# Three pairs of chunks block by block at a sub-layer's end, and the last output columns on other engines

## The chip, the cores and the metric

The kernel runs on one core of a Trainium2 chip. The metric is the time of one execution in device microseconds, the median of three runs. TensorE (PE in the profile, with PEld for its weight loads) multiplies matrices, VectorE (DVE), ScalarE (ACT) and GpSimd (POOL) work on the results, and SyncE (SP) issues the DMAs.

## The reference

A decoder trunk of two layers for 256 tokens of width 1024, in fp32. Each layer has an attention sub-layer (three head groups side by side) and an MLP sub-layer, and each sub-layer ends with a layer norm whose output the next sub-layer reads after a scale and a shift:

```
for l in range(DEPTH):                                   # DEPTH = 2
    mod = silu(c) @ ada_w[l] + ada_b[l]
    sh_a, sc_a, g_a, sh_m, sc_m, g_m = split(mod, 6)
    h = x * (1 + sc_a) + sh_a
    mixed = attention_groups(h @ w_in[l])                # A, B, C; width 1024
    x = layer_norm(DN_ALPHA * x + (1 + g_a) * (mixed @ w_out[l]), ln_g[l, 0], ln_b[l, 0])
    h = x * (1 + sc_m) + sh_m
    f = square(relu(h @ mlp_w1[l])) @ mlp_w2[l]          # 1024 -> 4096 -> 1024
    x = layer_norm(DN_ALPHA * x + (1 + g_m) * f, ln_g[l, 1], ln_b[l, 1])
return x
```

## The kernel before, in words

The 256 tokens are two blocks of 128 (`b` = 0, 1), the 1024 columns two halves of 512 (`h` = 0, 1). Every fp32 weight tile comes by a 1 MB DMA into one of four buffers (`raw`, issued in order by SP) and is split into a high part `whi` (ScalarE, L179) and a low part `wlo` (VectorE, or GpSimd where told, L180). A product is three matmuls: high by high, high by low, low by high. In the output projection these are `wo` (L1051 to L1053), in the MLP's second product `m2` (L1116 to L1118), each 128x512 into one of four accumulators. The split parts of a pair of chunks take four of the ten buffers `w` (128x1024 each); other pools are `u2` (eleven buffers of 128x512), `mx` (four, which also hold the MLP's activations), `P` (four) and `qk` (three).

A sub-layer ends in `transition`. The last two pairs of chunks are not done for both blocks in turn: block 0 gets its products half by half, then block 1 gets its own. While PE does block 1's, the other engines take block 0 through the norm. VectorE does `half(h)`: multiply (L405), add the residual (L409), statistics (L412); then mean and variance (L416 to L419), GpSimd's power (L420), the scaled row `P` (VectorE L427 for columns 0 to 511, ScalarE L425 and L426 for the rest), eight transposes on PE (`turn`, L454, tile `tp`), the modulation (VectorE L463, ScalarE L461), the high part of the new input `hT` (ScalarE L466) and its low part (VectorE L470). PE's next work after block 1's products is `v_tile` (L385, `mmv`), the first products of the next sub-layer for block 0, and it needs `hT`. Block 1's norm then runs beside these. Between the steps stand splits of weights for the next sub-layer: `pool_split` gives a `wlo` to GpSimd.

PE's order is made by the scheduler; the order on VectorE, ScalarE and GpSimd inside `transition` is the order of the code. This happens three times: at the end of layer 0's attention, of layer 0's MLP and of layer 1's attention. The end of layer 1's MLP is `last_norm`: block 0's last multiply and add run on GpSimd (`on_pool`, L539, 640 and then 384 columns), block 1's on VectorE (L563 and L566, two halves of 512), and SP stores the output (L535).

In the MLP the groups g = 0 to 15 of 256 inner columns follow one another: `m1(g+2)` makes activations ahead, `m2` uses those of g, and `filler` puts in steps of the next modulation vector (`gemv`: VectorE L234 on 1 MB of weights each).

Of the kernel before, what the change touches and what calls it, by code (L numbers as in the profile page):

```python
# [28 lines left out]
EARLY = 3  # L29
FO = (1, 3)  # L30
ORDER = ('kv0..21s4.3sa5.s.Acb.6.B7C..Ee', '.ts..q0412...ss3s.kva5cb.67AB.E..Ce')
GV = ('v', None, 'v', 'v', 'v')
# [88 lines left out]
def trunk_kernel(ctx: ExitStack, tc: tile.TileContext, a):  # L121
# [48 lines left out]

    SPARE = dict(P=4, qk=3, mx=4)

    def parts(t, n, eng=None, tag="w"):

        if tag == "w":
            hi, lo = (spl.tile([128, 1024], F32R, name=k, tag="w")[:, :n] for k in ("whi", "wlo"))
        else:
            hi, lo = (att.tile([128, 1024], F32R, name=k, tag=tag, bufs=SPARE[tag])[:, :n] for k in ("whi", "wlo"))
        nc.scalar.activation(hi, t, AF.Copy)  # L179
        (eng or nc.vector).tensor_tensor(lo, t, hi.bitcast(F32), op=OP.subtract)  # L180
        return hi, lo

    def split(t, rows, n):

        out = []
        for piece in pieces(t, rows, n, out):
            piece()
        return out

    def pieces(t, rows, n, out, step=None):  # L190
# [282 lines left out]
    def transition(products, accs, G, lnb, rnd, weights, spare, work):  # L473

        N = [Norm(b, accs[b], G, lnb) for b in range(2)]
        H = [MakeH(b, N[b], ROUND[rnd]) for b in range(2)]
# [52 lines left out]
    def last_norm(products, accs, G, lnb):  # L529

        N = [Norm(b, accs[b], G, lnb) for b in range(2)]
        E = mybir.EngineType

        def store(n, c0, c1):
            nc.sync.dma_start(a["out"][0, n.b * 128:(n.b + 1) * 128, c0:c1], x[:, n.b, c0:c1])  # L535

        def on_pool(n, c0, c1):
            for i, op in enumerate((OP.mult, OP.add)):
                nc.gpsimd.tensor_tensor(x[:, n.b, c0:c1], (n.r[:, c0:c1], x[:, n.b, c0:c1])[i], lnb[:, i, c0:c1], op=op)  # L539
            store(n, c0, c1)  # L540

        with tc.manual_schedule(engines={E.DVE, E.Pool}):
            n = N[0]
            for h in range(2):
                products(0, (h,))
# [7 lines left out]
            n = N[1]  # L553
            for h in range(2):
                products(1, (h,))
                n.half(h)
            n.stats()
            on_pool(N[0], 640, D)
            cuts = ((0, 512), (512, D))
            for c0, c1 in cuts:  # L560
                s = slice(c0, c1)
                o = n.halves[c0 // 512]
                nc.vector.scalar_tensor_tensor(o, o, n.mv[:, 0:1], lnb[:, 0, s], op0=OP.subtract, op1=OP.mult)  # L563
            for c0, c1 in cuts:
                s = slice(c0, c1)
                nc.vector.scalar_tensor_tensor(x[:, 1, s], n.halves[c0 // 512], n.ve[:, 1:2], lnb[:, 1, s],  # L566
                                               op0=OP.mult, op1=OP.add)
                store(n, c0, c1)

# [353 lines left out]
    for l in range(DEPTH):  # L923
# [119 lines left out]

        def wo(b, c2, hs):
            for k, h in ((k, h) for k in range(2) for h in hs):
                c = 2 * c2 + k
                hi, lo = WO[c]
                mh, ml = MX[c2][:, 0, k, b * 128:(b + 1) * 128], MX[c2][:, 1, k, b * 128:(b + 1) * 128]
                s = slice(h * 512, h * 512 + 512)
                o = accs[b][h]  # L1050
                nc.tensor.matmul(o, mh, hi[:, s], start=c == 0, stop=False)  # L1051
                nc.tensor.matmul(o, mh, lo[:, s], start=False, stop=False)  # L1052
                nc.tensor.matmul(o, ml, hi[:, s], start=False, stop=c == 7)  # L1053
# [51 lines left out]
        def load_w2(g):  # L1105
            W2[g] = split(rawload(a["mlp_w2"][l, g]), 2, 1024)

        def m2(g, b, hs):
            f = FT[g]
            t = slice(b * 128, (b + 1) * 128)  # L1110
            for i, h in ((i, h) for i in range(2) for h in hs):
                o = accs[b][h]
                s = slice(h * 512, h * 512 + 512)
                hi, lo = W2[g][i]
                first, lastk = g == 0 and i == 0, g == NG - 1 and i == 1
                nc.tensor.matmul(o, f[:, 0, i, t], hi[:, s], start=first, stop=False)  # L1116
                nc.tensor.matmul(o, f[:, 0, i, t], lo[:, s], start=False, stop=False)  # L1117
                nc.tensor.matmul(o, f[:, 1, i, t], hi[:, s], start=False, stop=lastk)  # L1118

        before = [p for g in range(EARLY) for p in w1_steps(g)]  # L1120
        end = transition(lambda b, h: [wo(b, c2, h) for c2 in (2, 3)], accs, ROUND[l, 3], lnb, (l, 2), before, SPARES[0],
                         [lambda b, g=g: m1_rows(g, b) for g in range(EARLY)])
# [4 lines left out]
        accs = [[ps.tile([128, 512], F32, name="m2", tag=t) for _ in range(2)] for t in ("acc", "sc")]  # L1127
        for g in range(NG - 2):
            with tc.issue_after(end[0]), tc.issue_after(end[1]):
                if EARLY <= g + 2 < NG:  # L1130
                    m1(g + 2)
                load_w2(g)
            for b in range(2):
                m2(g, b, (0, 1))
# [7 lines left out]
        tail = lambda b, h, m2=m2: [m2(g, b, h) for g in (NG - 2, NG - 1)]  # L1142
        if l < DEPTH - 1:
# [73 lines left out]
```

## Time and profile before

| | |
|---|---|
| median of 3 runs | 706.01 us (705.96 to 706.22) |
| the profiled execution | 706.43 us, of which its span 704.7 us |
| PE busy | 674.1 us, 96% of the span |
| VectorE, ScalarE, GpSimd busy | 492.3, 402.6, 39.1 us |
| mean granted TensorE clock | 0.991 of full speed |

The profile shows one execution. Busy times of PE overlap a little, since matmuls are pipelined: a 128x512 matmul is shown with 0.39 us, and one follows another after less.

### The profile page before, as it was taken

How to read it: one execution, taken by the hardware profiler on the slowest of the kernel's cores; microseconds unless marked ns; L12 is line 12 of the kernel's file. 1: busy time of each engine (PE TensorE's matmuls, PEld its weight loads, DVE VectorE, ACT ScalarE, POOL GpSimd, SP SyncE). 2: the span in 40 equal slices, each digit the busy share in tenths (PEclk: the TensorE clock that was granted, in tenths of full speed). 3: DMA queues.
4: the chain of work that ended last, by engine and by line, in shares of the span. 5: the costliest groups of instructions: out<-in, count | busy, mean ns of one | idle time of the engine just before them, and what ended most of it. 6: DMA issues, size and time to landing. Idle time of an engine off the chain costs nothing.

```text
span 704.7 us, 11146 instructions
## 1 busy us (share of the span) xinstructions
PE 674.1 (96%) x4284; PEld 550.9 (78%) x4284; DVE 492.3 (70%) x947; ACT 402.6 (57%) x781; POOL 39.1 (6%) x39
## 2 busy tenths in 40 slices
PE   5998899999999999999998999999999999999994
PEld 4898658458788888888878977867788888888883
DVE  3455965657799879798977976657779855555556
ACT  2345473785665546656555447598474655656550
POOL 0000000000400000000013020000220000000003
PEclk9999999999999999999999999999999999999998
DMA  9998686568459989798873757710538955555501
GB/s 337 350 353 312 224 319 231 169 236 312 162 183 363 346 309 344 283 344 327 326 262 120 282 226 274 272 39 23 183 117 294 373 214 195 212 183 180 180 0 60
DMA packets 29553, 167.68 MB, mean 238 GB/s; under 512 B 3199, under 2 KB 6683, under 8 KB 11964
## 3 DMA queue, kind: packets, MB, share of 16 engines
q1 hardware_dynamic: 29436, 166.94, 65.0%
q8 instruction: 34, 0.56, 0.3%
q14 instruction: 19, 0.16, 0.1%
q0 software_dynamic: 64, 0.02, 0.0%
HBM read 165.87 MB, written 1.08 MB: 237 GB/s over the span
## 4 chain that ended last, share of the span: by engine, by line
PE 89%; DVE 4%; ACT 3%; issue 1%; POOL 1%; DMA 1%; SPq 0%; POOLq 0%; DVEq 0%
PE mm L368 14%; PE m L1116 8%; PE m L1117 8%; PE m L1118 8%; PE mmv L385 7%; PE mm L369 7%; PE s L680 3%; PE tp L648 3%; PE gv L168 3%; PE mm L355 2%; PE mm L357 2%; PE mm L356 2%; PE wo L1051 2%; PE wo L1053 2%; PE acc L696 2%; PE wo L1052 2%
## 5 line engine op out<-in xcount | busy, mean ns | idle before, releaser
L180 DVE TENSOR_TENSOR wlo<-raw,whi 128x1024 fp32r<-128x1024 f32 (+2 forms) x166 | 196.8, 1203 | 56.5 <-ACT whi L179 54.9
L179 ACT ACTIVATE whi<-raw 128x1024 fp32r<-128x1024 f32 (+2 forms) x175 | 179.2, 1041 | 56.8 <-PE wo L1052 17.2
L368 PE MATMUL mm<-hT,whi 128*128 128x512 f32 x416 | 148.3, 398 | 0.0
L369 PE MATMUL mm<-hT,wlo 128*128 128x256 f32 x416 | 117.0, 281 | 0.9 <-DVE wlo L180 0.9
L1116 PE MATMUL m<-whi,mx 128*128 128x512 f32 x256 | 100.1, 391 | 0.0
L1117 PE MATMUL m<-wlo,mx 128*128 128x512 f32 x256 | 100.0, 391 | 0.0
L1118 PE MATMUL m<-whi,mx 128*128 128x512 f32 x256 | 99.5, 390 | 0.0
L368 PEld LDWEIGHTS mm<-hT,whi 128*128 128x128 f32 x416 | 78.2, 188 | 20.3 <-ACT whi L179 0.8
L369 PEld LDWEIGHTS mm<-hT,wlo 128*128 128x128 f32 x416 | 78.5, 189 | 2.5 <-DVE wlo L180 1.6
L234 DVE SCALAR_TENSOR_TENSOR qk<-raw,se,qk 128x1024 f32<-128x1024 f32 x56 | 71.4, 1286 | 2.5 <-DMA raw<-in_ada_dram 1.9
L371 ACT ACTIVATE P<-mm 128x256 f32<-128x256 f32 x52 | 19.7, 378 | 73.0 <-PE mm L369 73.0
L385 PE MATMUL mmv<-whi,hT 128*128 128x256 f32 (+2 forms) x352 | 55.9, 304 | 4.7 <-ACT hT L466 4.7
L1116 PEld LDWEIGHTS m<-whi,mx 128*128 128x128 f32 x256 | 48.1, 188 | 11.2 <-ACT whi L179 0.8
L1118 PEld LDWEIGHTS m<-whi,mx 128*128 128x128 f32 x256 | 48.1, 188 | 10.1
L1117 PEld LDWEIGHTS m<-wlo,mx 128*128 128x128 f32 x256 | 48.0, 188 | 8.9
L385 PEld LDWEIGHTS mmv<-whi,hT 128*128 128x128 f32 x352 | 48.8, 194 | 6.9 <-ACT hT L466 5.9
L636 ACT ACTIVATE P<-P,sxt 128x128 f32<-128x128 f32 (+1 forms) x96 | 42.6, 446 | 17.2 <-DVE sxt L634 17.0
L355 PE MATMUL mm<-hT,whi 128*128 128x256 f32 x128 | 37.4, 292 | 0.0
L357 PE MATMUL mm<-hT,wlo 128*128 128x256 f32 x128 | 37.0, 289 | 0.0
L356 PE MATMUL mm<-hT,whi 128*128 128x256 f32 x128 | 36.8, 287 | 0.0
L634 DVE CUSTOM_DVE_ANT_0 P<-s,bias 128x128 f32<-128x128 f32 (+1 forms) x80 | 25.7, 351 | 14.4 <-PE s L680 12.0
L1103 DVE TENSOR_TENSOR mx<-P,mx 128x512 fp32r<-128x512 f32 x26 | 17.9, 690 | 25.6 <-ACT mx L1102 25.6
(215 smaller groups left out, 1090.4 us busy)
## 6 DMA issues: line engine op xcount, KB each, us to landing
raw<-in_mlp_w_dram SPq DMA_DIRECT2D x64, 1024.0 KB, 6.5
raw<-in_ada_dram SPq DMA_DIRECT2D x32, 1024.0 KB, 5.9
raw<-in_adag_dram SPq DMA_DIRECT2D x16, 1024.0 KB, 6.7
raw<-in_w_in_dram SPq DMA_DIRECT2D x9, 1024.0 KB, 6.1
raw<-in_cmp_w_dram SPq DMA_DIRECT2D x8, 1024.0 KB, 6.8
raw<-in_w_out_dram SPq DMA_DIRECT2D x8, 1024.0 KB, 6.8
w<-in_w_in_dram SPq DMA_DIRECT2D x8, 396.0 KB, 7.2
w<-in_w_in_dram SPq DMA_DIRECT2D x8, 384.0 KB, 6.1
```

The lines of the kernel that those rows point to most:

```text
L179: nc.scalar.activation(hi, t, AF.Copy)
L180: (eng or nc.vector).tensor_tensor(lo, t, hi.bitcast(F32), op=OP.subtract)
L234: nc.vector.scalar_tensor_tensor(ac, src, by, ac, op0=OP.mult, op1=OP.add)
L355: nc.tensor.matmul(o[:, i], hi[:, c], hT[:, 0, kc], start=kc == 0, stop=False, skip_group_check=True)
L356: nc.tensor.matmul(o[:, i], hi[:, c], hT[:, 1, kc], start=False, stop=False, skip_group_check=True)
L357: nc.tensor.matmul(o[:, i], lo[:, c], hT[:, 0, kc], start=False, stop=kc == KC - 1, skip_group_check=True)
L368: nc.tensor.matmul(o, hi[:, c], hT[:, :, kc], start=kc == 0, stop=False, skip_group_check=True)
L369: nc.tensor.matmul(o[:, 0], lo[:, c], hT[:, 0, kc], start=False, stop=kc == KC - 1, skip_group_check=True)
L385: nc.tensor.matmul(o, hT[:, x_, kc, t], ws[kc][w_], start=kc == 0 and x_ + w_ == 0, stop=kc == KC - 1 and w_ == 1)
L1116: nc.tensor.matmul(o, f[:, 0, i, t], hi[:, s], start=first, stop=False)
L1117: nc.tensor.matmul(o, f[:, 0, i, t], lo[:, s], start=False, stop=False)
L1118: nc.tensor.matmul(o, f[:, 1, i, t], hi[:, s], start=False, stop=lastk)
```

## The change

The block-by-block part takes three pairs of chunks instead of two, so that each block has 36 matmuls there instead of 24. The additional pair's weights are split in pieces of 128x512 into eight `u2` buffers instead of four `w` buffers (`wide`). The transposes of block 0 stand, in the code, behind the seventh of block 1's twelve products (`TURN`). One `pool_split` before block 0's `scaled` goes away and the other comes behind it. The MLP's loop is shorter by one group, so that `m1` of groups 14 and 15 stand in one round, and the 21 steps of `filler` lie in 13 rounds (1, 2, 2, ...) instead of 14 (1, 2, ...). In `last_norm` GpSimd takes block 0 in halves of 512, and the last 192 columns of block 1 go through ScalarE and GpSimd in turn; the output leaves in five stores instead of four.

```diff
-    SPARE = dict(P=4, qk=3, mx=4)
+    SPARE = dict(P=4, qk=3, mx=4, u2=11)
...
+    def wide(t, small=False):
+        hs = [slice(0, 512), slice(512, 1024)]
+        if small:
+            return [[parts(t[:, i * 1024 + h * 512:i * 1024 + h * 512 + 512], 512, None, "u2") for h in range(2)]
+                    for i in range(2)]
+        return [[(hi[:, s], lo[:, s]) for s in hs] for hi, lo in split(t, 2, 1024)]
...
             for h in range(2):
-                products(0, (h,))
+                for p in products(0, (h,)):
+                    p()
                 N[0].half(h)
             N[0].stats()
+            N[0].scaled()
             pool_split()
-            pool_split()
-            N[0].scaled()
-            for jj in range(2):
-                H[0].turn(jj)
-            products(1, (0, 1))
+            for i, p in enumerate(products(1, (0, 1))):
+                p()
+                if i == TURN:
+                    for jj in range(2):
+                        H[0].turn(jj)
...
-            on_pool(n, 0, 640)
+                on_pool(n, h * 512, h * 512 + 512)
...
+            r = new_P().rearrange("p g k -> p (g k)")[:, :192]
+            nc.scalar.activation(r, m.halves[1][:, 320:], AF.Identity, bias=m.ve[:, 3:4])
+            nc.gpsimd.tensor_tensor(r, r, lnb[:, 0, 832:], op=OP.mult)
+            nc.scalar.activation(r, r, AF.Copy, scale=m.ve[:, 1:2])
+            nc.gpsimd.tensor_tensor(x[:, 1, 832:], r, lnb[:, 1, 832:], op=OP.add)
+            cuts = ((0, 512, m.halves[0]), (512, 832, m.halves[1][:, :320]))
...
-        for c2 in range(2):
-            WO.extend(split(rawload(a["w_out"][l, c2]), 2, 1024))
-            for b in range(2):
-                wo(b, c2, (0, 1))
-        for c2 in range(2, 4):
-            WO.extend(split(rawload(a["w_out"][l, c2]), 2, 1024))
+        WO += wide(rawload(a["w_out"][l, 0]))
+        for b in range(2):
+            for c, h in ((c, h) for c in range(2) for h in range(2)):
+                wo(b, c, h)
+        for c2 in range(1, 4):
+            WO += wide(rawload(a["w_out"][l, c2]), c2 == 1)
...
-        for g in range(NG - 2):
+        for g in range(NG - 3):
...
-                filler(1 + g % 2)
+                filler(1 + (g % 3 > 0))
...
-        for g in (NG - 2, NG - 1):
+        for g in (NG - 3, NG - 2, NG - 1):
             load_w2(g)
```

VectorE at the end of layer 0's attention, before (numbers are the program's buffers; `wo_1765` and `wo_1766` are block 0's two halves, `raw_1857` and `raw_1859` the first weights of the MLP):

```order
L180 TENSOR_TENSOR wlo_1850<-raw_1847,whi_1849 128x1024
L180 TENSOR_TENSOR wlo_1870<-raw_1857,whi_1869 128x1024
L180 TENSOR_TENSOR wlo_1854<-raw_1847,whi_1853 128x1024
L180 TENSOR_TENSOR wlo_1866<-raw_1857,whi_1865 128x1024
L180 TENSOR_TENSOR wlo_1874<-raw_1859,whi_1873 128x1024
L405 TENSOR_TENSOR wo_1765<-wo_1765,G_1332 128x512
L409 SCALAR_TENSOR_TENSOR wo_1765<-x_101,wo_1765 128x512
L412 BN_STATS st_1863<-wo_1765 128x6
L405 TENSOR_TENSOR wo_1766<-wo_1766,G_1332 128x512
```

And the same place now (`raw_1841` and `raw_1843` are the MLP's first weights):

```order
L182 TENSOR_TENSOR wlo_1818<-raw_1803,whi_1817 128x512
L182 TENSOR_TENSOR wlo_1834<-raw_1831,whi_1833 128x1024
L182 TENSOR_TENSOR wlo_1838<-raw_1831,whi_1837 128x1024
L182 TENSOR_TENSOR wlo_1854<-raw_1841,whi_1853 128x1024
L182 TENSOR_TENSOR wlo_1850<-raw_1841,whi_1849 128x1024
L415 TENSOR_TENSOR wo_1765<-wo_1765,G_1332 128x512
L419 SCALAR_TENSOR_TENSOR wo_1765<-x_101,wo_1765 128x512
L182 TENSOR_TENSOR wlo_1858<-raw_1843,whi_1857 128x1024
L422 BN_STATS st_1847<-wo_1765 128x6
L415 TENSOR_TENSOR wo_1766<-wo_1766,G_1332 128x512
```

A split of the MLP's weights now stands between the sums and the statistics of block 0's first half, and all splits of the output projection lie ahead of that half.

PE at the end of layer 0's MLP, before (`m_2222` and `m_2223` are block 1's halves, `tp` the transposes of block 0, `mmv` the next layer's first products):

```order
L1118 MATMUL m_2222<-whi,mx 128x512
L454 MATMUL tp<-p_78,P 128x128 x4
L1116 MATMUL m_2223<-whi,mx 128x512
L1117 MATMUL m_2223<-wlo,mx 128x512
L454 MATMUL tp<-p_78,P 128x128 x4
L1118 MATMUL m_2223<-whi,mx 128x512
L385 MATMUL mmv<-whi,hT 128x280 x12
```

The same place now (`m_2230` and `m_2231` are block 1's halves):

```order
L1129 MATMUL m_2231<-whi,mx 128x512
L464 MATMUL tp<-p_78,P 128x128 x8
L1130 MATMUL m_2231<-wlo,mx 128x512
L1131 MATMUL m_2231<-whi,mx 128x512
L1129 MATMUL m_2230<-whi,mx 128x512
```

The eight transposes now stand together behind 22 of block 1's 36 matmuls, with 14 after them; before, three matmuls of block 1 stood behind the first of them. At the end of layer 0's attention 25 stand ahead of them and 11 behind.

GpSimd at the end of the program, before (`x<-P,lnb` is the multiply, `x<-x,lnb` the add, `ve<-ve,co` the power):

```order
L539 TENSOR_TENSOR x<-P,lnb 128x640
L539 TENSOR_TENSOR x<-x,lnb 128x640
L420 TENSOR_TENSOR ve<-ve,co 128x1
L539 TENSOR_TENSOR x<-P,lnb 128x384
L539 TENSOR_TENSOR x<-x,lnb 128x384
```

And now:

```order
L553 TENSOR_TENSOR x<-P,lnb 128x512
L553 TENSOR_TENSOR x<-x,lnb 128x512
L430 TENSOR_TENSOR ve<-ve,co 128x1
L576 TENSOR_TENSOR P<-P,lnb 128x192
L578 TENSOR_TENSOR x<-P,lnb 128x192
```

All of block 0 now comes ahead of block 1's power, and behind it only 192 columns of block 1.

## Rows read from the trace of the kernel before

**Rows 1.** The page: the chain that ended last, by engine

```profile
PE 89%; DVE 4%; ACT 3%; issue 1%; POOL 1%; DMA 1%; SPq 0%; POOLq 0%; DVEq 0%
```

**Rows 2.** Waits of PE, by line: us in total, times, longest

```profile
PE mmv L385 <- ACT hT L466: 4.7, 3, 2.2
```

**Rows 3.** Timeline of PE, layer 0's attention end: start, duration, instruction, [idle before]

```profile
162.60 0.39 PE L1052 MATMUL wo<-wlo,mx 128*128 128x512 f32 x1
...
175.32 0.39 PE L1051 MATMUL wo<-whi,mx 128*128 128x512 f32 x1
...
183.70 2.89 PE L385 MATMUL mmv<-whi,hT 128*128 128x256 f32 x22 [1.26 <-ACT hT L466]
...
190.29 1.03 PE L454 MATMUL tp<-p,P 128*128 128x128 f32 x8
```

**Rows 4.** Timeline of PE, layer 0's MLP end

```profile
373.00 4.05 PE L385 MATMUL mmv<-whi,hT 128*128 128x280 f32 x21 [2.19 <-ACT hT L466]
```

**Rows 5.** Timeline of PE, end of layer 1's attention

```profile
484.31 0.50 PE L1051 MATMUL wo<-whi,mx 128*128 128x512 f32 x1
...
487.14 0.39 PE L1053 MATMUL wo<-whi,mx 128*128 128x512 f32 x1
...
512.04 2.88 PE L385 MATMUL mmv<-whi,hT 128*128 128x256 f32 x22 [1.26 <-ACT hT L466]
```

**Rows 6.** Windows: length, busy by engine, granted PE clock, DMA share, GB/s

```profile
183.70:192.00 8.30, 8.30 (x68) 8.00 (x69) 6.70 (x14) 4.55 (x10) 2.96 (x2) 1.00 0.57 209
...
372.00:374.00 2.00, 1.00 (x8) 1.01 (x9) 1.11 (x3) 2.00 (x4) 0.70 (x1) 1.00 0.96 385
374.00:376.00 2.00, 2.00 (x13) 2.00 (x12) 2.00 (x4) 0.38 (x1) 1.55 (x1) 0.59 0.20 82
376.00:378.00 2.00, 2.00 (x11) 2.00 (x11) 1.86 (x6) 0.00 (x0) 0.83 (x1) 0.56 0.27 49
```

**Rows 7.** Timeline of VectorE, end of layer 0's attention

```profile
175.52 0.70 DVE L405 TENSOR_TENSOR wo<-wo,G 128x512 f32<-128x512 f32 x1
...
178.85 0.81 DVE L427 TENSOR_SCALAR P<-wo,mv,ve 128x512 f32<-128x512 f32 x1 [0.68 <-POOL ve L420]
```

**Rows 8.** The page: costliest groups: busy, mean ns of one | idle before, releaser

```profile
L180 DVE TENSOR_TENSOR wlo<-raw,whi 128x1024 fp32r<-128x1024 f32 (+2 forms) x166 | 196.8, 1203 | 56.5 <-ACT whi L179 54.9
```

**Rows 9.** Timeline of ScalarE, end of layer 0's attention

```profile
160.06 0.59 ACT L246 ACTIVATE rs<-gv 128x512 f32<-128x512 f32 x1
...
178.01 1.06 ACT L179 ACTIVATE whi<-raw 128x1024 fp32r<-128x1024 f32 x1 [0.30 <-PE wo L1052]
...
179.29 0.78 ACT L426 ACTIVATE P<-wo,ve 128x512 f32<-128x512 f32 x1
181.31 1.82 ACT L461 ACTIVATE tp<-tp,sb 128x128 f32<-128x128 f32 x4 [1.25 <-PE tp L454]
```

**Rows 10.** Weight loads of line L138: time from issue to landing, all of them

```profile
DMA to landing us min/median/max: 3.5/6.6/10.7
```

**Rows 11.** Window in layer 0's MLP, columns as in the windows above

```profile
300.00:320.00 20.00, 20.00 (x109) 16.42 (x109) 18.73 (x25) 10.69 (x16) 0.00 (x0) 1.00 0.94 356
```

**Rows 12.** Timeline of the last ten microseconds, all engines (SPq: issues on SP's queue)

```profile
694.40 0.39 PE L1118 MATMUL m<-whi,mx 128*128 128x512 f32 x1
...
697.40 1.41 DVE L563 SCALAR_TENSOR_TENSOR m<-m,mv,lnb 128x512 f32<-128x512 f32 x2
697.60 0.55 POOL L420 TENSOR_TENSOR ve<-ve,co 128x1 f32<-128x1 f32 x1
...
698.72 1.40 DVE L566 SCALAR_TENSOR_TENSOR x<-m,ve,lnb 128x512 f32<-128x512 f32 x2
699.18 0.99 POOL L539 TENSOR_TENSOR x<-x,lnb 128x384 f32<-128x384 f32 x1
...
700.59 0.93 SPq L535 DMA_DIRECT2D out_dram<-x  x2
```

**Rows 13.** The output's stores: KB each, median us from issue to landing

```profile
out_dram<-x SPq DMA_DIRECT2D x2, 256.0 KB, 2.3
```

More of the change, by code (lines that the diff above doesn't have):

```diff
@@ L30 @@
 FO = (1, 3)
+TURN = 6
 ORDER = ('kv0..21s4.3sa5.s.Acb.6.B7C..Ee', '.ts..q0412...ss3s.kva5cb.67AB.E..Ce')
@@ L177, in parts @@
         else:
-            hi, lo = (att.tile([128, 1024], F32R, name=k, tag=tag, bufs=SPARE[tag])[:, :n] for k in ("whi", "wlo"))
+            m = 512 if tag == "u2" else 1024
+            hi, lo = (att.tile([128, m], F32R, name=k, tag=tag, bufs=SPARE[tag])[:, :n] for k in ("whi", "wlo"))
         nc.scalar.activation(hi, t, AF.Copy)
@@ L540, in on_pool @@
             store(n, c0, c1)
+        n, m = N
         with tc.manual_schedule(engines={E.DVE, E.Pool}):
-            n = N[0]
             for h in range(2):
-                products(0, (h,))
+                for p in products(0, (h,)):
+                    p()
                 n.half(h)
@@ L551, in last_norm @@
                 nc.scalar.activation(n.r[:, h * 512:h * 512 + 512], n.halves[h], AF.Identity, bias=n.ve[:, 2:3], scale=n.ve[:, 1:2])
-            on_pool(n, 0, 640)
-            n = N[1]
+                on_pool(n, h * 512, h * 512 + 512)
             for h in range(2):
[L555 to L568, printed above, removed]
+                for p in products(1, (h,)):
+                    p()
+                m.half(h)
+            m.stats()
+            r = new_P().rearrange("p g k -> p (g k)")[:, :192]
[4 more added lines that the diff above has]
+            cuts = ((0, 512, m.halves[0]), (512, 832, m.halves[1][:, :320]))
+            for c0, c1, o in cuts:
+                nc.vector.scalar_tensor_tensor(o, o, m.mv[:, 0:1], lnb[:, 0, c0:c1], op0=OP.subtract, op1=OP.mult)
+            for c0, c1, o in cuts:
+                nc.vector.scalar_tensor_tensor(x[:, 1, c0:c1], o, m.ve[:, 1:2], lnb[:, 1, c0:c1], op0=OP.mult, op1=OP.add)
+                store(m, c0, c1)
+            store(m, 832, D)
     bias = cst.tile([128, 12, 256], F32, name="bias")
@@ L1042, in trunk_kernel, with wo @@
         WO = []
[L1044 to L1053, printed above, removed]
-        for c2 in range(2):
-            WO.extend(split(rawload(a["w_out"][l, c2]), 2, 1024))
-            for b in range(2):
-                wo(b, c2, (0, 1))
-        for c2 in range(2, 4):
-            WO.extend(split(rawload(a["w_out"][l, c2]), 2, 1024))
+        def wo(b, c, h):
+            c2, k = divmod(c, 2)
+            hi, lo = WO[c][h]
+            mh, ml = MX[c2][:, 0, k, b * 128:(b + 1) * 128], MX[c2][:, 1, k, b * 128:(b + 1) * 128]
+            o = accs[b][h]
+            nc.tensor.matmul(o, mh, hi, start=c == 0, stop=False)
+            nc.tensor.matmul(o, mh, lo, start=False, stop=False)
+            nc.tensor.matmul(o, ml, hi, start=False, stop=c == 7)
+        WO += wide(rawload(a["w_out"][l, 0]))
[4 more added lines that the diff above has]
+            WO += wide(rawload(a["w_out"][l, c2]), c2 == 1)
         NG = FF // 256
@@ L1105, in load_w2, with m2 @@
         def load_w2(g):
-            W2[g] = split(rawload(a["mlp_w2"][l, g]), 2, 1024)
-        def m2(g, b, hs):
+            W2[g] = wide(rawload(a["mlp_w2"][l, g]), g == NG - 3)
+        def m2(g, i, b, h):
             f = FT[g]
             t = slice(b * 128, (b + 1) * 128)
[L1111 to L1118, printed above, removed]
+            o = accs[b][h]
+            hi, lo = W2[g][i][h]
+            first, lastk = g == 0 and i == 0, g == NG - 1 and i == 1
+            nc.tensor.matmul(o, f[:, 0, i, t], hi, start=first, stop=False)
+            nc.tensor.matmul(o, f[:, 0, i, t], lo, start=False, stop=False)
+            nc.tensor.matmul(o, f[:, 1, i, t], hi, start=False, stop=lastk)
         before = [p for g in range(EARLY) for p in w1_steps(g)]
-        end = transition(lambda b, h: [wo(b, c2, h) for c2 in (2, 3)], accs, ROUND[l, 3], lnb, (l, 2), before, SPARES[0],
+        end = transition(lambda b, hs: [lambda c=c, h=h: wo(b, c, h) for c in range(2, 8) for h in hs], accs,
+                         ROUND[l, 3], lnb, (l, 2), before, SPARES[0],
                          [lambda b, g=g: m1_rows(g, b) for g in range(EARLY)])
@@ L1131, in trunk_kernel @@
                     m1(g + 2)
+                if g == NG - 4:
+                    m1(NG - 1)
                 load_w2(g)
             for b in range(2):
-                m2(g, b, (0, 1))
+                for i, h in ((i, h) for i in range(2) for h in range(2)):
+                    m2(g, i, b, h)
             with tc.issue_after(end[1]):
@@ L1137, in trunk_kernel @@
                     end[2][g].keep(nc.vector)
-                filler(1 + g % 2)
+                filler(1 + (g % 3 > 0))
         filler(100)
-        for g in (NG - 2, NG - 1):
+        for g in (NG - 3, NG - 2, NG - 1):
             load_w2(g)
-        tail = lambda b, h, m2=m2: [m2(g, b, h) for g in (NG - 2, NG - 1)]
+        tail = lambda b, hs, m2=m2: [lambda g=g, i=i, h=h: m2(g, i, b, h)
+                                         for g in (NG - 3, NG - 2, NG - 1) for i in range(2) for h in hs]
         if l < DEPTH - 1:
```

## The prediction

> **What bounds the kernel now.** I read the chain that ended last first: PE holds 89% of it, VectorE and ScalarE 7% together [rows 1]. So time is won only where PE stands still or its clock is low. The list of PE's waits shows where that happens for the work of this change: the matmul `mmv` waits three times for ScalarE's `hT`, 4.7 us in all [rows 2]. The timelines of PE place the three at the sub-layer ends: 1.26 us [rows 3], 2.19 us [rows 4] and 1.26 us [rows 5]. The windows show what follows the long one: the granted clock falls to 0.59 and 0.56 for 4 us, the lower of the two levels (1.2 GHz) for most of it [rows 6]. The fourth thing to read is the end of the program, where PE has stopped and the other engines and the stores run alone [rows 12].
>
> What a gap consists of is a race. At the end of layer 0's attention PE begins block 1 at 175.32, and VectorE begins block 0's second half at 175.52 [rows 3, 7]. From that multiply to the first `mmv` at 183.70 take 8.18 us. In the same time PE has 24 matmuls; from 162.60 to 175.32 lie 56 steps of one matmul, 0.227 us each, so they are 5.45 us, and the eight transposes 1.03 [rows 3]. With 36 matmuls PE has 8.18 + 1.03 = 9.21 us of its own. If VectorE begins on time, the chain of 8.18 us fits and no gap is left, at each of the three places.
>
> **End of layer 0's MLP.** The gap of 2.19 us goes. Block 1 would begin at t and have its products and transposes done at t + 9.21; VectorE's multiply stands at t + 0.2. One new wait lies in the chain: a split (1.2 us [rows 8]) stands between the mean and `P`, and its buffer is released by block 1's twelfth matmul at t + 2.9. It ends at t + 4.2; `P` would have begun at t + 3.53 (178.85 - 175.32), so it ends at t + 5.05 instead of t + 4.35. The transposes stand behind 22 matmuls, at t + 5.0, so PE does not wait. ScalarE then modulates for 1.82 us and writes the first `hT` in some 0.6, near t + 8.6. The gap is gone and its price is 2.2 us. The clock is the second term: (1 - 0.59) x 2 + (1 - 0.56) x 2 = 1.7 us of full-speed work is missing in the two windows [rows 6]. After both gaps of 1.26 us the clock shows no such fall (the window from 183.70 to 192 has 1.00), so without a gap I expect none. Part of the 1.7 us may be hidden, since block 1's `hT` comes only when VectorE has finished block 1's norm; I take 1.3 (bounds 0 and 1.7). Together 3.5, bounds 2.2 and 3.9.
>
> A rule speaks against putting the transposes together. The Trainium skill, "TensorE: Matmul & The Clock Gate", section "Part 4: PE-mode transpose", says that transposes do not count as PE activity in the same way as matmuls. By it eight in a row would be a pause for the clock; the row shows eight in a row at 190.29 and the clock at 1.00 in the window around it [rows 3, 6], so the trace does not bear the rule out at this length, and by the rule the sum would lack the 1.3 us.
>
> **End of layer 0's attention.** Here VectorE is not on time. All splits of the last three pairs must now be done ahead of block 0's first half. The 128x512 pieces wait for ScalarE, which ends `rs` at 160.65 [rows 9]; the first piece ends on VectorE near 161.9, and then follow three more of some 0.7 us (a 128x512 operation [rows 7]), six of 1.2 [rows 8] and small work of about 0.9 us, so that the multiply of half 0 begins near 172.4. PE loses only some 0.3 us, because it has matmuls of the first pair and of half 1 in between: thirteen first-pair products after 162.06, then 36 of block 0, which brings block 1's begin to about 173.5. But VectorE's half 0 (0.7 + 0.7), the split that now stands in it (1.2) and its statistics (0.7) put the multiply of half 1 at 175.75, 2 us later than PE allows. Add 8.18: 183.93. The transposes standing together save some 0.5 (the second four followed after two matmuls), and the ScalarE split of 1.06 between `P` and the modulation [rows 9], where it was ahead of `P` before, adds some 0.4. `mmv` begins near 183.85, as before: PE's longer cover is eaten by VectorE's lateness. The split in the middle also waits for a weight load, issued only when the pair in small pieces has been split, near 167.6. A load lands in 3.5 us at the least, 6.6 in the median [rows 10]; 5 would cost nothing, 6.6 costs 1.5, and I take 5 to 5.5, since the load ahead of it is issued some 11 us earlier. Term: 0.3 us lost, bounds 2.0 lost and 0.9 won (if VectorE keeps PE's pace).
>
> **End of layer 1's attention.** The gap of 1.26 goes, since the splits come earlier there. But matmuls of the second pair filled PE between transposes of the attention before (eight from 484.31 to 487.14, 1.8 us [rows 5]), and with the small buffers split last they are no longer there: they move behind, and PE stands still for about 1.2 us instead. Won 0.1, bounds 0.8 lost and 0.9 won.
>
> **The MLP of layer 0.** The same 21 steps lie in one round less. A round has 48 matmul slots, 11 us. VectorE has four splits, 4.8, and about 1.5 of other work, and each step two instructions of 1.28, so a round with two steps has 11.4 us. One in two was hidden; now two follow each other. VectorE is busy for 18.73 of 20 us in the fullest window [rows 11]. PE's matmuls have buffers ahead, so I take 0.3 lost, bounds 0 and 1.0.
>
> **The end.** PE's last matmul ends at 694.79 and the last store is issued at 701.06 (the second of the pair from 700.59 on [rows 12]). SP stood behind GpSimd's 384 columns, done at 700.17. Now block 0 is done early; behind the power (until 698.15) GpSimd has 192 columns twice, each 192 x 2.58 ns = 0.5 (from 0.99 for 384), with a ScalarE step of about 0.3 between: 699.55. VectorE's 512 and 320 columns twice end at 699.7. The issues, 0.47 apart, begin near 699.6, the last near 700.5. That is 0.6 earlier, and fewer bytes are left: 512 KB instead of 704, which is 0.5 us at the 385 GB/s of a full window [rows 6]. A store lands in 2.3 us [rows 13], which stays. Won 0.8, bounds 0.6 and 1.2.
>
> **The sum.** 3.5 - 0.3 + 0.1 - 0.3 + 0.8 = 3.8 us. Against the profiled execution of 706.43 (span 704.7 and 1.73 around it) that is 702.6; the median lay 0.42 below the profiled one, so 702.2 for the median.
>
> **Rivals.**
> First, VectorE keeps PE's pace at both attention ends: 0.9 won at each, 0.8 kept in the end, nothing lost in the MLP: 3.5 + 0.9 + 0.9 + 0.8 = 6.1, or 6.5 with the end's upper bound: 699.5. For it speaks that VectorE had idle times before splits (54.9 us of waiting for ScalarE [rows 8]); against it that these splits wait on ScalarE too.
> Second, the change does little: the gaps only move to other places at the attention ends (1.8 and 0.8 lost) and the MLP loses 1.0; 3.5 + 0.8 - 3.6 = 0.7 won, 705.3.
> Third, the clock does not recover at the MLP's end, by the transposes or a short gap: 1.3 less, 703.5. Against it stand the windows after 1.26 us.
> Fourth, on the other side: the splits placed into the statistics wait for loads. At the attention's end a landing after 7.5 us (issue 167.6) puts the multiply of half 1 at 178.1 and loses 3.0; at the MLP's end the same would have to arrive 2.5 us late, and then the whole 3.5 is gone, for `P` is on the path with nothing behind it on VectorE. With 0.5 lost at each of the other two places and 0.8 won: 3.2 lost, 709.2. It decides from landings of about 7 us on at both places; the median of 6.6 [rows 10] holds it near, the early issue at the MLP's end speaks against it.
>
> **How the numbers follow.** Forecast 0.46, first rival 0.24, second 0.14, third 0.08, fourth 0.08. The forecast alone lies between 701.0 and 703.4. The range of 699.0 to 705.6 leaves out about 0.08 of the first, 0.04 of the second and the fourth. 0.2% is 1.4 us, about what a measurement here tells from no change. Faster than 704.6: forecast, first, third and a fifth of the second, 0.81. Slower than 707.4: the fourth, 0.07. The same: 0.12.
>
> **What would show it.** PE's list of waits: `mmv` for `hT` falls from 4.7 us to about 0.5 to 1.5, all of it at the end of layer 0's attention. The windows behind the MLP's end show the clock at 1.00. The timeline of VectorE there shows the split between L419 and L422; if its idle time is longer than 0.5 us, the load is late. In layer 1's attention PE shows new idle time near 490. The last issue of SP lies 5.7 us behind PE's last matmul instead of 6.3. I am wrong if new waits of PE for `wlo` or `whi` of the output projection exceed 2 us, or if the clock stays low.

## Result, and the profile after

The changed kernel takes 701.54 us (median of four runs, 700.93 to 701.95) against 706.12 us for the kernel before beside it: a ratio of 0.9934, 95% interval 0.9922 to 0.9947, so it is faster by 4.6 us (3.7 to 5.5). Its profiled execution took 700.93 us, with a span of 699.2 us.

The first thing to look at is PE's list of waits in the changed kernel (us in total, times, longest), and above it the chain that ended last:

```profile
PE 88%; DVE 4%; ACT 3%; DMA 2%; issue 1%; SPq 0%; POOL 0%; POOLq 0%; DVEq 0%; ACTq 0%
```

```profile
PE gv L169 <- DMA raw<-in_ada_dram: 6.4, 1, 6.4
PE mm L341 <- ACT hT L319: 2.7, 4, 1.6
...
PE mm L379 <- DVE wlo L182: 1.2, 3, 0.5
PE acc L790 <- ACT pT L667: 0.8, 1, 0.8
...
PE tp L464 <- DVE P L437: 0.2, 1, 0.2
```

The wait of `mmv` for `hT` [rows 2] is no longer in it: all three gaps are closed. Two prices stand there instead: `mm` for `wlo` has gone from two waits to three, and `acc` for `pT` is new, 0.76 us. A second wait has shrunk that belongs to the same race. In the kernel before, the same list has

```profile
PE tp L454 <- DVE P L427: 0.8, 2, 0.4
```

which is 0.38 us ahead of the first four transposes of block 0 at each of the two attention ends. Both are gone; the 0.2 that is left stands elsewhere, ahead of block 1's transposes behind the MLP's end.

**End of layer 0's attention.** PE's timeline (start, duration, instruction, idle before) answers to [rows 3]; VectorE's and ScalarE's to [rows 7, 9]:

```profile
178.36 1.09 PE L464 MATMUL tp<-p,P 128*128 128x128 f32 x8
181.88 3.01 PE L395 MATMUL mmv<-whi,hT 128*128 128x256 f32 x23
```

```profile
163.02 1.22 DVE L182 TENSOR_TENSOR wlo<-raw,whi 128x1024 fp32r<-128x1024 f32 x1
164.15 0.16 DVE L281 TENSOR_TENSOR sb<-sb,md 128x8 f32<-128x8 f32 x1
164.23 6.96 DVE L182 TENSOR_TENSOR wlo<-raw,whi 128x512 fp32r<-128x512 f32 x7
171.11 0.69 DVE L415 TENSOR_TENSOR wo<-wo,G 128x512 f32<-128x512 f32 x1
171.84 0.70 DVE L419 SCALAR_TENSOR_TENSOR wo<-x,wo 128x512 f32<-128x512 f32 x1
172.44 1.22 DVE L182 TENSOR_TENSOR wlo<-raw,whi 128x1024 fp32r<-128x1024 f32 x1
173.57 0.69 DVE L422 BATCH_NORM_STATS2 st<-wo 128x6 f32<-128x512 f32 x1
174.18 0.68 DVE L415 TENSOR_TENSOR wo<-wo,G 128x512 f32<-128x512 f32 x1
```

```profile
170.79 1.06 ACT L181 ACTIVATE whi<-raw 128x1024 fp32r<-128x1024 f32 x1 [2.03 <-DMA raw<-in_mlp_w_dram]
...
179.49 1.82 ACT L471 ACTIVATE tp<-tp,sb 128x128 f32<-128x128 f32 x4
181.24 1.07 ACT L476 ACTIVATE hT<-tp 128x512 fp32r<-128x512 f32 x2
```

The reader is to see three things. The last seven of VectorE's ten splits run back to back (in 6.96 us), half 0 begins at 171.11 and half 1 at 174.18. The load that the split inside the statistics needs has landed by 170.79, 1.65 us before VectorE comes to that split; only ScalarE, which had nothing else to do, waited for it. And `hT`, begun at 181.24, is there just as PE ends its 36 matmuls at 181.88.

**End of layer 0's MLP.** PE's timeline, VectorE's at the scaled row `P`, and the windows (columns as in [rows 6]) answer to [rows 4] and [rows 6]:

```profile
365.11 1.09 PE L464 MATMUL tp<-p,P 128*128 128x128 f32 x8
369.23 2.94 PE L395 MATMUL mmv<-whi,hT 128*128 128x280 f32 x22
```

```profile
363.10 1.22 DVE L182 TENSOR_TENSOR wlo<-raw,whi 128x1024 fp32r<-128x1024 f32 x1
364.25 0.80 DVE L437 TENSOR_SCALAR P<-m,mv,ve 128x512 f32<-128x512 f32 x1
```

```profile
370.00:372.00 2.00, 2.00 (x18) 2.00 (x17) 2.00 (x5) 0.01 (x1) 1.86 (x1) 1.00 0.96 406
372.00:374.00 2.00, 2.00 (x19) 2.00 (x18) 1.90 (x4) 0.78 (x3) 0.54 (x1) 1.00 0.16 61
374.00:376.00 2.00, 1.83 (x16) 1.63 (x15) 1.16 (x4) 1.61 (x4) 1.59 (x2) 1.00 0.00 0
```

No idle time stands ahead of `mmv`. The split of a weight that stands ahead of `P` holds it back until 364.25, but `P` is there at 365.05 and PE comes to the transposes at 365.11. The granted clock is 1.00 (the level of 2.4 GHz) in each window, where it was 0.59 and 0.56 for 4 us behind the gap before.

**End of layer 1's attention.** The gap is closed here too ([rows 5] has it with 1.26 us). PE now stands still earlier, among the transposes of the attention; the first row is a wait still earlier in this layer, which comes up below:

```profile
431.96 0.42 PE L855 MATMUL cv<-gK,p 128*64 128x16 f32 x8 [0.33 <-DVE gK L845]
...
480.52 1.03 PE L665 MATMUL tp<-p,P 128*128 128x128 f32 x8
482.32 0.43 PE L790 MATMUL acc<-pT,vab 128*64 128x128 f32 x2 [0.76 <-ACT pT L667]
...
502.73 1.09 PE L464 MATMUL tp<-p,P 128*128 128x128 f32 x8
...
507.09 1.12 PE L395 MATMUL mmv<-whi,hT 128*128 128x256 f32 x8
```

**The end.** The last microseconds, all engines, answer to [rows 12]:

```profile
689.57 0.39 PE L1131 MATMUL m<-whi,mx 128*128 128x512 f32 x1
...
693.80 0.45 ACT L577 ACTIVATE P<-P,ve 128x192 f32<-128x192 f32 x1 [0.70 <-POOL P L576]
694.34 0.59 POOL L578 TENSOR_TENSOR x<-P,lnb 128x192 f32<-128x192 f32 x1 [0.56 <-ACT P L577]
```

```profile
691.54 4.70 SPq L549 DMA_DIRECT2D out_dram<-x  x4
```

GpSimd is done at 694.93, 4.97 us behind PE's last matmul (689.96); before, it was 5.38 us behind it. SP's last issue ends at 696.24, 6.28 us behind PE; before, 6.73.

**A table by stretch.** The first 111 us of the span, which none of the kernels here changes, took 110.5 to 112.0 us in the thirteen traces (111.06 and 111.66 in the two of the changed kernel), so I compare stretches that begin and end at a PE instruction found in every trace: a product `cv` of the attention at 111 us, the first `mmv` of each sub-layer end, the start of the last `m`, and the span's end.

```
                        to mmv of      to mmv of    to mmv of      to the    to the
                        layer 0's      layer 0's    layer 1's      last m    span's
                        attention end  MLP end      attention end            end
before                  72.68          189.30       139.04         182.36    10.30
after                   70.82          187.35       137.86         182.48     9.63
after, a second trace   70.85          187.51       137.38         182.48     9.62
```

So 1.85 us come from layer 0's attention end, 1.8 to 1.95 from its MLP end, 1.2 to 1.7 from the stretch that holds both the clock behind the MLP's end and layer 1's attention end, and 0.7 from the end of the program. The two traces of the changed kernel differ by 0.48 us in the third stretch: in the first, PE waits 0.33 us at 431.96 for `gK`, a tile that VectorE writes, and in the second it doesn't. The profiled pair differs by 5.5 us, more than the medians' 4.6: the profiled execution of the changed kernel was the fastest of its four, and that of the kernel before lay 0.3 above its median.

### The profile page after: what moved, and what is told of

Its sections match the earlier page's. It is cut to its first block, busy times and chain, and to the rows that moved or that the text cites. A ratio compares the mean times of both kernels' runs of the same rounds, so it can differ in the third digit from the quotient of the medians.

```text
span 699.2 us, 11153 instructions
## 1 busy us (share of the span) xinstructions
PE 672.6 (96%) x4284; PEld 549.5 (79%) x4284; DVE 490.3 (70%) x955; ACT 401.7 (57%) x791; POOL 41.0 (6%) x41
## 4 chain that ended last, share of the span: by engine, by line
PE 88%; DVE 4%; ACT 3%; DMA 2%; issue 1%; SPq 0%; POOL 0%; POOLq 0%; DVEq 0%; ACTq 0%
PE mm L378 14%; PE mmv L395 8%; PE m L1129 8%; PE m L1130 8%; PE m L1131 8%; PE mm L379 7%; PE gv L169 3%; PE s L697 2%; PE mm L365 2%; PE wo L1066 2%; PE mm L367 2%; PE wo L1068 2%; PE tp L665 2%; PE wo L1067 2%; PE mm L366 2%; PE mm L341 2%
## 5 line engine op out<-in xcount | busy, mean ns | idle before, releaser
L182 DVE TENSOR_TENSOR wlo<-raw,whi 128x1024 fp32r<-128x1024 f32 (+3 forms) x174 | 196.6, 1154 | 49.7 <-ACT whi L181 48.1
L181 ACT ACTIVATE whi<-raw 128x1024 fp32r<-128x1024 f32 (+3 forms) x183 | 178.5, 1002 | 32.8 <-PE mm L378 14.5
L395 PE MATMUL mmv<-whi,hT 128*128 128x256 f32 (+2 forms) x352 | 54.5, 299 | 0.0
L430 POOL TENSOR_TENSOR ve<-ve,co 128x1 f32<-128x1 f32 x8 | 4.4, 552 | 548.1 <-DVE ve L429 443.6
```

The lines of the kernel that those rows point to most:

```text
L395: nc.tensor.matmul(o, hT[:, x_, kc, t], ws[kc][w_], start=kc == 0 and x_ + w_ == 0, stop=kc == KC - 1 and w_ == 1)
```

## The experiments

Theory A was my prediction's account with each part's gain at its place: the MLP's end carries the change by its gap and the clock. Rival B was that the gain sits at the attention ends (the prediction's first rival). The first two kernels keep one part of the change each, and the third takes one part back.

**Only the MLP's end.** The attention ends and the code of the last norm are as before; in layer 0's MLP the third pair, the small buffers, the moved transposes and the split remain.

```diff
-        WO += wide(rawload(a["w_out"][l, 0]))
+        for c2 in range(2):
+            WO += wide(rawload(a["w_out"][l, c2]))
...
-        for c2 in range(1, 4):
-            WO += wide(rawload(a["w_out"][l, c2]), c2 == 1)
+        for c2 in range(2, 4):
+            WO += wide(rawload(a["w_out"][l, c2]))
```

> Three pairs block by block at the two MLP ends only; the attention ends and the last norm as before. Theory (the 2.2 us gap and the low clock behind it were the larger part of the gain): 3.4 us won at the end of layer 0's MLP, 0.2 lost in its loop, so about 702.9 against 706.1, and the clock 1.00 behind that end. Rival (the clock's loss was hidden by block 1's norm): only the gap, about 704.1.

Measured: 704.06 us (702.92 to 704.67, seven runs), ratio 0.9972 (0.9961 to 0.9982). By the trace the stretch to the MLP's `mmv` is 187.54 us, as in the changed kernel, and the gaps of 1.26 and 1.28 us at the attention ends are back. The MLP's part is worth 1.9 us (1.3 to 2.8), not the 3.2 of theory A. The clock is at 1.00 behind the MLP's end (372 to 380), and yet the stretch from there to the next `mmv` is 138.36 us, only 0.7 less than before; in this trace PE waits 0.49 us for `gK` in it, for which it doesn't wait in the kernel before.

**Only the attention ends.** The MLP of both layers and the program's end are as before.

```diff
-            W2[g] = wide(rawload(a["mlp_w2"][l, g]), g == NG - 3)
+            W2[g] = wide(rawload(a["mlp_w2"][l, g]), False)
...
-        for g in range(NG - 3):
+        for g in range(NG - 2):
...
-                filler(1 + (g % 3 > 0))
+                filler(1 + g % 2)
```

> Three pairs at the two attention ends only; MLP and last norm as before. Theory from the trace of the changed kernel: 1.8 us won at the end of layer 0's attention and about 0.3 at that of layer 1, less about 0.4 that the layer 1 attention lost on its way for another reason, so about 704.0 to 704.4; the gap and the low clock at the MLP's end are still there. Rival (the prediction's sum): 0.2 us lost at both together, about 706.3.

Measured: 704.54 us (702.82 to 705.29, eight runs), ratio 0.9975 (0.9965 to 0.9985). The stretch to the first `mmv` is 70.82 us, exactly that of the changed kernel: its 1.86 us come from this part alone. The gap of 2.20 us at the MLP's end is there. So the attention ends are worth 1.1 to 2.5 us, about as much as the MLP's end, and neither account holds alone. Of the eight executions six took 704.27 to 705.29 us at a mean clock of 0.990 or 0.991, and two took 702.82 and 703.08 at 0.993. The profiled one, of the six, shows the fall behind the gap (0.57 from 372 to 376). By their mean clock the other two had a fall less; which one, a mean can't tell.

**The old end of the program.** The last norm as before, all else as changed.

```diff
-                on_pool(n, h * 512, h * 512 + 512)
+            on_pool(n, 0, 640)
...
-            r = new_P().rearrange("p g k -> p (g k)")[:, :192]
...
+            on_pool(N[0], 640, D)
+            cuts = ((0, 512), (512, D))
```

> The changed kernel with the last norm of before. Theory: 0.7 us of the gain come from the end, so about 702.2. Rival: with three pairs block 0 is out of GpSimd's way anyway and the new last columns bring nothing, about 701.5.

Measured: 701.93 us (700.91 to 704.25, six runs), ratio 0.9943 (0.9930 to 0.9956), 0.4 us above the changed kernel; in the trace 10.25 us pass from the last `m` to the end of the span, against 9.63. The new end is worth 0.6 us by the trace; the medians can't separate it from nothing.

**The clock without the gap's other cost.** The kernel before, with eight extra 128x512 matmuls (on data already there, into an unused bank) in the gap at the MLP's end; it computes something more, and nothing of the reference is left out.

```diff
+            with tc.issue_after(end):
+                for i in range(8):
+                    nc.tensor.matmul(o, f[:, 0, 1, 128:256], hi[:, 512:1024], start=i == 0, stop=i == 7)
```

> The kernel before with eight extra 128x512 matmuls into a free accumulator in the 2.19 us gap at the end of layer 0's MLP (their result is not used). Theory: the gap stays in length, but the clock behind it stays at 1.00, and 1.2 us are won: about 704.9. Rival 1: the clock's loss lay beside block 1's norm, no gain, 706.1. Rival 2: the clock falls all the same.

Measured: 705.65 us (704.53 to 706.39, eleven runs), ratio 0.9992 (0.9983 to 1.0001). PE's timeline at the MLP's end:

```profile
371.66 1.99 PE L1152 MATMUL warm<-whi,mx 128*128 128x512 f32 x8
374.02 2.17 PE L385 MATMUL mmv<-whi,hT 128*128 128x280 f32 x15 [0.37 <-ACT hT L466]
```

In this trace the clock stays up behind it (1.00 in the windows from 372 to 378), and the stretch from this `mmv` to the next is 137.62 us instead of 139.04: 1.4 us, the size of my term. The median moved by 0.3 us (a gain of 1.2 to a loss of 0.1). Both theories are hit by half: in the pair of traces the fall costs 1.4 us, but the median hardly moves. This profiled execution had a fall of its own at 80 us (below), which the profiled one of the kernel before had not. That the clock falls behind the MLP's end in only some executions of the kernel before would explain the median, and is not shown. It leaves the mean worth of the clock term open between 0 and 1.2 us.

**What each piece of the change carries.** Four kernels take one piece out of the changed one, to see which of the pieces the closed gaps need. The transposes last:

```diff
-TURN = 6
+TURN = 11
```

> The changed kernel with the transposes behind all of block 1's products (TURN = 11). Theory (the gap is a race between PE's own products and the chain transposes, modulation, hT): PE has nothing left to do after the transposes, a gap of 2.4 us at each of the three sub-layer ends, 7 us in all, and the clock low behind some of them, another 1 to 4: 709 to 713. Rival (the three pairs alone close the gap, the transposes' place is of no matter): 701.5.

Measured: 711.18 us (709.05 to 711.56, six runs), ratio 1.0060 (1.0048 to 1.0073), 9.6 us above the changed kernel. PE at the three ends, and windows behind each:

```profile
184.32 1.92 PE L395 MATMUL mmv<-whi,hT 128*128 128x256 f32 x14 [2.43 <-ACT hT L476]
...
374.27 1.98 PE L395 MATMUL mmv<-whi,hT 128*128 128x280 f32 x8 [2.43 <-ACT hT L476]
...
515.17 2.89 PE L395 MATMUL mmv<-whi,hT 128*128 128x256 f32 x22 [2.43 <-ACT hT L476]
```

```profile
186.00:188.00 2.00, 2.00 (x19) 2.00 (x19) 1.97 (x4) 0.00 (x0) 2.00 (x1) 1.00 0.13 49
...
374.00:376.00 2.00, 1.73 (x8) 1.73 (x9) 1.75 (x3) 1.65 (x3) 0.22 (x1) 0.65 0.38 160
376.00:378.00 2.00, 2.00 (x11) 2.00 (x10) 1.97 (x4) 0.00 (x0) 2.00 (x1) 0.50 0.00 0
...
516.00:518.00 2.00, 2.00 (x19) 2.00 (x18) 2.00 (x4) 0.55 (x1) 1.37 (x1) 1.00 0.19 78
```

Three equal gaps make 7.3 us. The other 2.3 fit the clock, whose mean was 0.987 to 0.991 in these six executions and 0.991 to 0.995 in those of the changed kernel. The gaps stay closed only with the transposes in the middle of block 1's products, where matmuls behind them cover ScalarE's work.

Ordinary buffers for the third pair:

```diff
-            WO += wide(rawload(a["w_out"][l, c2]), c2 == 1)
+            WO += wide(rawload(a["w_out"][l, c2]))
...
-            W2[g] = wide(rawload(a["mlp_w2"][l, g]), g == NG - 3)
+            W2[g] = wide(rawload(a["mlp_w2"][l, g]))
```

> The changed kernel with the third pair's weights in four w buffers instead of eight small ones. Theory: ten w buffers don't hold three pairs (twelve), so block 0 waits for block 1's first products, the norm of block 0 begins when block 1's products are nearly done, and a gap of more than 3 us with a low clock behind it stands at all three ends: 712 or more. Rival (buffers come free in time): 701.5 to 703.

Measured: 725.91 us (723.87 to 726.76, five runs), ratio 1.0275 (1.0261 to 1.0290). PE at layer 0's attention end:

```profile
182.46 1.09 PE L464 MATMUL tp<-p,P 128*128 128x128 f32 x8 [1.29 <-DVE P L437]
185.98 1.35 PE L395 MATMUL mmv<-whi,hT 128*128 128x256 f32 x8 [2.43 <-ACT hT L476]
```

Without buffers of its own the third pair takes those of the splits that follow. At this end ScalarE then waits 3.22 us, until 172.61, for a matmul of the output projection to release one; VectorE begins half 0 at 176.21 instead of 171.11, and `P` and `hT` come late. The same stands at the other two ends (1.93 and 1.28 us for `P`, 2.43 each for `hT`), 11.8 us together. In four microseconds behind each gap (186 to 190, 380 to 384, 524 to 528) the granted clock is 0.61, 0.50 and 0.50, by which I estimate 5.6 us of full-speed work lost, and at the program's end 15.4 us pass from PE's last matmul to the end instead of 9.2. That makes 23.6 of the 24 us. The stretches of the table leave no remainder: they are 4.1, 6.5, 4.4, 2.9 and 6.1 us longer than those of the changed kernel's first trace, 24.0 together.

Both of GpSimd's splits ahead of the scaling, as before the change:

```diff
+            pool_split()
+            pool_split()
             N[0].scaled()
-            pool_split()
```

> The changed kernel with both weight splits ahead of block 0's scaled row, as before the change. Theory: the second of them waits on ScalarE for a buffer that block 1's products release late, P on ScalarE comes some 1 to 2 us later, the second four transposes move behind more products, and a gap of 0.5 to 2 us comes back at each of three ends: 703 to 707. Rival (the buffer is free in time): 701.5.

Measured: 706.90 us (706.32 to 709.43, twelve runs), ratio 1.0016 (1.0007 to 1.0025), 5.4 us above the changed kernel. PE's gaps:

```profile
184.09 2.17 PE L395 MATMUL mmv<-whi,hT 128*128 128x256 f32 x16 [1.28 <-ACT hT L476]
...
373.43 2.80 PE L395 MATMUL mmv<-whi,hT 128*128 128x280 f32 x20 [1.73 <-ACT hT L476]
...
512.75 2.88 PE L395 MATMUL mmv<-whi,hT 128*128 128x256 f32 x22 [1.74 <-ACT hT L476]
```

At layer 0's attention end ScalarE's half of `P` begins 1.82 us behind VectorE's (180.14 against 178.32), in the changed kernel 0.33: ScalarE makes the high parts of both splits first, and had to wait until 177.50 for a matmul of block 1 before the first of them. So the second four transposes stand at 181.06, 1.88 us behind the first four, instead of next to them. That is 4.75 us of gaps for two splits that stand ahead of one step; this move, a line in the diff, is worth as much as the whole change. My prediction had priced it only by ScalarE's split that now stands between `P` and the modulation, as 0.4 us lost.

The old pattern of the steps in the MLP:

```diff
-                filler(1 + (g % 3 > 0))
+                filler(1 + g % 2)
```

> The changed kernel with the old pattern of one and two steps in the MLP loop; two of the 21 steps are then left for behind the loop. Theory (the loop lost 0.2 us by pairs of full rounds in a row): the loop 0.2 shorter, but the steps left over stand on VectorE ahead of the sub-layer's end and cost more than that: 701.5 to 704. Rival: nothing measurable.

Measured: 704.64 us (703.94 to 705.03, nine runs), ratio 0.9976 (0.9966 to 0.9985), 3.1 us above the changed kernel. PE near the end of layer 0's MLP:

```profile
352.50 0.66 PE L271 MATMUL tp<-p,rs 128*128 128x128 f32 x4 [0.72 <-ACT rs L256]
...
369.89 1.07 PE L464 MATMUL tp<-p,P 128*128 128x128 f32 x8 [0.50 <-DVE P L437]
...
373.39 1.80 PE L395 MATMUL mmv<-whi,hT 128*128 128x280 f32 x12 [0.61 <-ACT hT L476]
```

With the old pattern two of the 21 steps are left for behind the loop. Transposes of a step (`tp<-p,rs`) are then still waited for near its end, VectorE's `P` comes 0.50 us late, and the gap is back in part. The stretch to this `mmv` takes 190.71 us, 3.2 to 3.4 more than in the changed kernel, which is the whole loss. The denser pattern, which costs 0.2 to 0.4 us in the loop, is needed.

**A better place for the small buffers.** The wait of 0.76 us for `pT` is the price that the prediction had named: matmuls of the second pair were no longer there between the transposes. The next two kernels give the small buffers to the fourth pair of the output projection, in layer 1 alone and in both layers; beside them the changed kernel ran once more.

```diff
-            WO += wide(rawload(a["w_out"][l, c2]), c2 == 1)
+            WO += wide(rawload(a["w_out"][l, c2]), c2 == (1, 3)[l])
```

> The changed kernel, but in layer 1's attention the small buffers hold the fourth pair instead of the second, so that products of the second pair can again stand between the transposes of the attention. If the wait there (0.76 us of idle PE for pT at 482.32 in the changed kernel) was the price of putting the second pair into the small buffers, it goes, and the time is 700.7 to 701.1 (0.4 to 0.8 us under 701.5); the distance from layer 0's last mmv wait to layer 1's falls from 137.9 to about 137.2. The rival is that the splits in the statistics then come at another place and PE waits for P or hT instead: 701.5 to 702.5, with mmv idle by 0.3 to 1 us.

```diff
-            WO += wide(rawload(a["w_out"][l, c2]), c2 == 1)
+            WO += wide(rawload(a["w_out"][l, c2]), c2 == 3)
```

> The same in both layers: the small buffers hold the fourth pair of the output projection. At layer 0's attention end the transposes of block 0 and hT had no slack in the changed kernel. If VectorE's eight small splits at the end (0.60 us each) take the same time as the four wide ones (1.14 each), layer 0's end is unchanged (70.8 us from the first kv projection marker to mmv) and the time is that of layer 1's variant, 700.7 to 701.1. The rival is that the small splits, each a separate wait for ScalarE, delay block 0's first half: a gap of 0.3 to 1.2 us ahead of mmv at layer 0, and 701.3 to 702.3.

> The changed kernel once more, unaltered, for a median over more executions beside the two variants: 701.5 if the first four executions stood for it (700.9 to 702.0); where the clock's fall behind block ends differs between executions, single ones up to 1 us above or below.

Measured: 699.79 us (698.75 to 701.82, six runs), ratio 0.9907 (0.9892 to 0.9922) for layer 1 alone; 699.91 us (699.37 to 700.44, four runs), ratio 0.9908 (0.9893 to 0.9922) for both; 701.50 us (699.97 to 701.89, six runs), ratio 0.9926 (0.9911 to 0.9940) for the changed kernel again. PE in layer 1's attention, small buffers last there alone:

```profile
479.69 0.38 PE L665 MATMUL tp<-p,P 128*128 128x128 f32 x2
...
480.14 0.82 PE L665 MATMUL tp<-p,P 128*128 128x128 f32 x6
...
482.04 0.43 PE L790 MATMUL acc<-pT,vab 128*64 128x128 f32 x2
...
504.60 1.60 PE L395 MATMUL mmv<-whi,hT 128*128 128x256 f32 x12
```

The wait for `pT` is gone: matmuls of the output projection stand among the transposes, no new idle time stands ahead of `P` or `hT`, and from the layer's first `mmv` to this one pass 135.78 us (136.04 with both layers) instead of 137.4 to 137.9. That is 1.3 to 2.1 us, more than the 0.4 to 0.8 that I expected. 0.76 of it is the named wait. Another 0.45 are two more matmuls of the output projection among the next transposes: seven stand there in 3.16 us, where the changed kernel's second trace has five in 3.15. I did not trace the rest. With this order layer 1's attention end wins as much as layer 0's: 135.78 us is 1.84 less than the 137.62 of the warmed kernel, which has the old attention ends and no fall of the clock in this stretch. At layer 0's attention end both orders take the same (70.62 and 70.85 us), as expected. The intervals of the ratios overlap, so the 1.6 to 1.7 us between the medians rest on the traces, where both variants show them.

## Why the prediction came out as it did

The time lay 0.7 us under the forecast and inside its range, and part of that is luck: one term had the wrong sign and was off by 2.2 us. In the profiled pair the gain is 5.5 us instead of 3.8, mostly by this term. In the medians it is 4.6; the 0.9 between the two lies in which executions were profiled.

**The race at the MLP's end** was right, step by step: the gap of 2.19 us is gone and nothing has taken its place. With block 1's begin (t) at 360.13, the split ahead of `P` ends at t + 4.2 as forecast, `P` at t + 4.9 (forecast 5.05), and the transposes begin at t + 5.0 without a wait.

**The clock term** of 1.3 us was right for an execution in which the clock falls (1.4 by the stretches of the warmed kernel), and is not shown as a fixed price. In the kernel with only the attention ends changed, two executions of eight had a fall less by their mean clock. What the change wins by it in the median is bounded by the warmed kernel (0 to 1.2) and not settled.

**Layer 0's attention end** is the step that was mis-sized: I took 0.3 us lost and it won 1.86. The prediction let half 1's multiply begin at 175.75; it began at 174.18. The largest part of these 1.6 us lies in the price of a split: I took 1.2 and 0.7 us, the durations in the rows, but instructions that follow each other overlap in their records, and the pitch is 1.14 and 0.60 (seven of them, five wide and two small, in 6.96 us). Over the nine splits that I summed this makes 0.7 us; the small work between them was 0.25 us less than I took, half 0 itself (174.18 - 171.11) 0.2 us less, and the rest was rounding up. The chain from there to `mmv` then took 7.70 us instead of the 8.1 that I had put together (183.85 - 175.75): eight transposes together, with ScalarE's split behind `P`, saved 0.46 and not 0.1. What I had listed as the first rival, VectorE keeping PE's pace, is what happened here, with no slack at all: `hT` arrives as PE is ready for it. But the rival's price of 0.9 won was too low by half as well. It counted the gap ahead of `mmv` alone and left out the 0.38 us that PE had waited for `P` ahead of the first four transposes; the two together are 1.64 of the 1.86.

**Layer 1's attention end.** Named rightly, gap against new idle time: 1.26 us won and, left out again, 0.38 ahead of the transposes; 0.76 lost at `pT`, and a remainder of 0.5 lost. Between the kernel before and the one with only the attention ends changed, both with a fall of the clock, this stretch differs by 0.37 us; I took 0.1. That the loss comes from where the small buffers are given is shown by the two last kernels.

**The MLP loop** lost 0.2 to 0.4 us (the stretch shrinks by 1.8 to 1.95 where the gap was 2.19); 0.30 of it is the third wait for `wlo`, at 265.69, which the kernel with the old pattern doesn't have. I took 0.3. **The end** won 0.7 of the 0.8.

**The rivals.** The first was right at layer 0's attention end and not at layer 1's. The second (gaps only move) holds for 0.76 us in layer 1. The third falls: after eight transposes in a row the windows show 1.00 at each of the three ends. The rule of the Trainium skill that stood beside it ("TensorE: Matmul & The Clock Gate", section "Part 4: PE-mode transpose") is neither borne out nor refuted by that: the eight take 1.03 to 1.09 us, and PE standing still for 1.26 us at the attention ends of the kernel before left the clock at 1.00 too. No run here shows longer rows of transposes. The fourth falls by ScalarE's row: the load had landed by 170.79, ahead of the split.

What I had not priced is how much hangs on single pieces: taking back GpSimd's splits costs 5.4 us and the step pattern 3.1, more than the whole gain of 4.6 and two thirds of it. Nothing in my sum showed how close the chain is to opening again.

## What to carry to other kernels

Where an engine works through a row of like instructions, price them by the distance of their starts in a packed group, not by the duration of one; over nine of them this made 0.7 us here, in a race that was won with no slack. A gap closes only if every link of the chain behind it is early enough: take out one link at a time, and look for the idle time that the cover's old place now shows. If buffers are to be given to one of several like pieces, give them to one whose work fills nothing elsewhere.

## What the runs showed of the hardware

A fall of the granted clock is not fixed by the length of the gap before it. In the kernel with the transposes last, three gaps of 2.43 us stood in one execution, at three places of the program; behind the first and third the windows show 1.00, behind the second 0.65 and 0.50. A gap of 1.8 us at 79 us of the span stands in all thirteen traces, in code that none of the kernels changes; a fall follows it in two of them and not in the other eleven. The window behind it, first in the changed kernel, then in the warmed one:

```profile
80.00:84.00 4.00, 4.00 (x25) 4.00 (x24) 4.00 (x12) 1.68 (x5) 0.00 (x0) 1.00 0.96 328
```

```profile
80.00:84.00 4.00, 4.00 (x16) 4.00 (x15) 3.78 (x10) 1.47 (x5) 0.00 (x0) 0.57 0.98 342
```

PE starts 25 matmuls there at the one clock and 16 at the other. From the gap to the product `cv` at 111 us pass 33.5 us in the two traces with the fall and 31.9 in the eleven without, so this fall costs 1.6 us; the one behind the MLP's end cost 1.4. Such falls may be a good part of the spread of 1 to 2 us between executions of one kernel. What decides whether one comes, these runs don't show.
